# A projection's plain weight quarter in the tiles of the second sum, and a new order of the final norm's factors and the accumulators' additions

## The chip, the cores and the metric

One core of one Trainium2 chip runs the program alone. The metric is the device time in microseconds (us). Engines are named as in the profile: PE is TensorE, PEld its weight loads, DVE VectorE, ACT ScalarE, POOL GpSimd, SP SyncE, which only issues DMAs.

## What is computed

Two decoder layers on 512 tokens of width 1024, in float32: a pooling mixer and a latent attention of 16 heads, each with a SiLU gate and an output projection, plain residual additions, and one last RMSNorm. The change lies in the last projection and that norm:

```python
y = o.reshape(B, S, MLA_WIDTH) * jax.nn.silu(z)   # 512 x 2048
x = x + y @ w_out                                 # w_out: 2048 x 1024
return rmsnorm(x, final_norm)
```

## The kernel before

Every product of float32 matrices is made of three products of halves (`hi` and `lo`, a rounded part and the rest): `mm3` at L183 to L185. The halves of a weight strip come from ACT (`hi`, a copy) and DVE (`lo`, a subtraction): L166 and L167 for plain strips, L559 and L560 for summed ones, L188 and L189 for the activations.

The last projection is done in seven products instead of eight. `y` is cut into a11, a12, a21, a22 (two halves of the 2048 inner rows by two halves of the tokens), `w_out` into four quarters (two halves of the inner rows by LEFT and RIGHT columns). Some products take a quarter of `w_out` as it is, others a sum of quarters. Two objects of the class `Summed` hold these sums: `x_sum` in eight tiles (256 KB each) and `y_sum` in four (512 KB each). Their `load` fetches a quarter on SP's queue, or adds one to what the tiles hold, by an accumulating DMA on POOL's queue (L546). Their `strip(i)` makes the `hi` and `lo` of half a quarter. All strips, plain or summed, are cut from one ring of four buffers, two for a strip (`hi` and `lo`), so two strips live at a time. A plain strip (`columns_of`) goes through a ring of five `raw` buffers of 256 KB.

`products()` and `finish()`, under a hand-written order (`tc.manual_schedule()`), hold the work after the attention's last head, and the lines of each engine run in the order in which they stand. Ahead of them the heads' loop is put in order by the compiler's scheduler. One product (a11 with the plain upper LEFT quarter, into `acc`) is made in the heads' loop. Then six sets of products follow each other on PE; the first five are calls `multiply(banks, strips, slot, start)` of 48 matmuls, the last one is written out in `finish()` as calls of `part`:

1. both, with t1 (x_sum) and s1
2. last, with p2 (the plain quarter: lower half of the inner rows, LEFT) and a12
3. acc, with t2 (x_sum) and s2
4. both again, with y1 (y_sum) and s2 + a12
5. acc again, with y2 (y_sum) and s3
6. acc again, with t4 (x_sum) and a22

`acc`, `both` and `last` are pairs of PSUM banks, one bank for each of two token tiles. A later set adds to what a bank holds, so `gather` (L610, DVE), which adds a bank to the residual `xs`, must have read the bank between two sets. `split_rows` makes the halves of a part of y in `slots[0]` or `slots[1]`; `combine_rows` (L1055) forms s1, s2, s3.

y_sum's four tiles take the place of attention tiles: two `pm` buffers (the softmax's rows, last read by the transposes, L1022), `pt_hi` and `pt_lo` (last read by the values product, L183 to L185 and L1044). The output rows `o` later take the same four places.

The last norm: `square(t, c)` (ACT, L1210) sums the squares of half a token tile, `total` and `power` (POOL, L1218, L1226, L1227) make the factor `rs`, `normed` (DVE, L1233) multiplies and `send` stores on SP.

Of the kernel before, what the change touches and what calls it, by code (L numbers as in the profile page):

```python
# [11 lines left out]
F32 = mybir.dt.float32  # L12
# [3 lines left out]
ALU = mybir.AluOpType  # L16
# [34 lines left out]
def trunk_kernel(  # L51
# [514 lines left out]
    def columns_of(w, half, c, i):  # L566

        return strip([(w_rows(w, half * 8 + 4 * i, 4)[:, :, c], 4, 512)])[0]
# [32 lines left out]
    def multiply(banks, strips, slot, start, then=None):  # L601
        for q in range(2):
            for t in range(2):
                part(banks[t], strips[q], slot, q, t, start and q == 0, q == 1, not start)
                if then and q == 1:
                    then(t)

    def gather(t, c, b, op=ALU.add):

        dve.tensor_tensor(xs[:, t, c], xs[:, t, c], b, op)  # L610
# [420 lines left out]
    def values(h):  # L1031
        st, i2 = pairs[h // 2], h % 2
        c = slice(i2 * DN, (i2 + 1) * DN)
        b = bank()
        for j in range(NT - 1):
            n = S - j * P
            mm3(
                b[:, j * P :],
                tuple(v[:, j, c] for v in st["v"]),
                tuple(t[:, PT_BASE[j] : PT_BASE[j] + n] for t in (pt_hi, pt_lo)),  # L1040
                j == 0,
                False,
            )
        pe.matmul(b[:, S - P :], st["v3"][:, c], pt_3, start=False, stop=True)  # L1044
        dve.tensor_tensor(y[:, h, :], b, y[:, h, :], ALU.mult)
# [7 lines left out]
    def combine_rows(out, a, b, op, k0, k1):  # L1053
        for k in range(k0, k1, 2):
            dve.tensor_tensor(*(v[:, k : k + 2, :] for v in (out, a, b)), op)  # L1055

    def split_rows(src, slot, k0, k1):
        halves(*(v[:, k0:k1, :] for v in (src, *slot)))
# [14 lines left out]
    def first_sum(k0, k1):  # L1073
# [2 lines left out]
        x_sum.load(0, LEFT, pieces=range(k0, k1))  # L1076
        x_sum.load(0, RIGHT, add=True, pieces=range(k0, k1))

    (k0, q0), (k1, q1), vs = projections(0)
    qr = {1: QRope(1)}  # L1080
    k0()
# [10 lines left out]
    for h in range(H):  # L1092
        p, odd = divmod(h, 2)
        g, t = divmod(h + 5, 4)
        if h == 12:
            slots[1] = slot_of((lp, "t2"), (lp, "q_r"))
            first_half[0] = columns_of(w_out2, 0, LEFT, 0)
            split_rows(a11, slots[1], 0, 4)
            acc = [bank() for _ in range(2)]
        if h == 13:  # L1100
            split_rows(a11, slots[1], 4, 8)
        nxt = scores(h + 1) if h + 1 < H else None
        if h == 13:
            first_sum(0, 7)
        if h == 14:
            first_sum(7, 8)
        if odd:
            ahead = projections(p + 2) if p + 2 < H // 2 else [[], [], []]
        transposes(sc[0])
        if nxt:  # L1110
            softmax(*nxt)
        if units[odd]:
            units[odd][0]()
        if units[odd]:
            units[odd][1]()
        if h >= 12:
            q, t_ = divmod(h - 12, 2)
            part(acc[t_], first_half[q], slots[1], q, t_, q == 0, q == 1, False)
        if h == 14:
            slots[0] = slot_of((lp, "latT_hi"), (wk, "q_r"))  # L1120
            s1 = lp.tile([P, 8, 256], F32, name="s1", tag="latT_lo", bufs=1)
            combine_rows(s1, a21, a22, ALU.subtract, 0, 6)
            split_rows(s1, slots[0], 0, 4)
        if h == 15:
            t1 = [x_sum.strip(0)]
            split_rows(s1, slots[0], 4, 6)
        values(h)
        if g < 4 and t < 2:
            if t == 0:
                qr[g] = QRope(g)  # L1130
            qr[g].half(t)
            if t == 1:
                qr[g].turn()
        if odd:
            for u in units[2]:
                u()
            units = ahead
        if h == 13:
            first_half[1] = columns_of(w_out2, 0, LEFT, 1)
        sc = nxt  # L1140
# [3 lines left out]
    combine_rows(a21, a11, a21, ALU.subtract, 0, 6)  # L1144
    combine_rows(a11, s1, a11, ALU.subtract, 0, 6)
    s3, s2 = a21, a11
    y_sum.tiles = [
        ap.tile([P, 2, S], F32, name="b_y", tag=tag, bufs=n)
        for tag, n in (("pm", 2), ("pm", 2), ("pt_hi", 1), ("pt_lo", 1))
    ]  # L1150
    both = [bank() for _ in range(2)]
    last = [bank() for _ in range(2)]
    g_fin = row(final_norm, D, "g_fin", tag="gain")
# [1 line left out]
    def products():  # L1155

        combine_rows(s1, a21, a22, ALU.subtract, 6, 8)
        split_rows(s1, slots[0], 6, 8)
        x_sum.load(1, RIGHT, add=True, pieces=range(4))
        t1.append(x_sum.strip(1))  # L1160
        x_sum.load(1, RIGHT, add=True, pieces=range(4, 8))
        multiply(both, t1, slots[0], True)
        split_rows(a12, slots[1], 0, 4)
        p2 = [columns_of(w_out2, 1, LEFT, 0)]
        split_rows(a12, slots[1], 4, 8)
        p2.append(columns_of(w_out2, 1, LEFT, 1))
        y_sum.load(1, RIGHT)
        multiply(last, p2, slots[1], True)
        for t in range(2):
            gather(t, LEFT, acc[t])  # L1170
            gather(2 + t, RIGHT, both[t])
        combine_rows(s3, a11, a21, ALU.subtract, 6, 8)
        combine_rows(s2, s1, a11, ALU.subtract, 6, 8)
        split_rows(s2, slots[0], 0, 4)
        split_rows(s2, slots[0], 4, 8)
        t2 = x_sum.strips()
        x_sum.load(1, LEFT, add=True)
        multiply(acc, t2, slots[0], False)
        for i in (0, 4):
            combine_rows(s2, s2, a12, ALU.add, i, i + 4)  # L1180
            split_rows(s2, slots[1], i, i + 4)
        y1 = [y_sum.strip(0)]
        for t in range(2):
            gather(t, LEFT, last[t])
        y1.append(y_sum.strip(1))
        y_sum.load(0, RIGHT, add=True)
        multiply(both, y1, slots[1], False)
        for t in range(2):
            gather(t, RIGHT, acc[t], ALU.subtract)
        split_rows(s3, slots[0], 0, 4)  # L1190
        split_rows(s3, slots[0], 4, 8)
        y2 = [y_sum.strip(0)]
        for t in range(2):
            gather(t, RIGHT, both[t])
        y2.append(y_sum.strip(1))
        multiply(acc, y2, slots[0], False)
        split_rows(a22, slots[1], 0, 4)
        split_rows(a22, slots[1], 4, 8)

    o = [  # L1200
        ap.tile([P, D], F32, name="o", tag=tag, bufs=n)
        for tag, n in (("pm", 2), ("pm", 2), ("pt_hi", 1), ("pt_lo", 1))
    ]
    junk = lp.tile([P, 512], F32, name="junk", tag="k_a", bufs=1)
    ssq = {t: [] for t in range(NT)}
    rs = {}
# [1 line left out]
    def square(t, c):  # L1208
        r = sm.tile([P, 1], F32, name="ssq", tag="ssq8", bufs=12)
        act.activation(  # L1210
            junk[:, : c.stop - c.start], xs[:, t, c], AF.Square, scale=D**-0.5, accum_out=r
        )
        ssq[t].append(r)

    def total(t):

        r = sm.tile([P, 1], F32, name="total")
        pool.tensor_scalar(r, ssq[t][0], EPS, None, ALU.add)  # L1218
        for q in ssq[t][1:]:
            pool.tensor_tensor(r, r, q, ALU.add)  # L1220
        ssq[t] = [r]

    def power(t):

        rs[t] = sm.tile([P, 1], F32, name="rs")
        pool.tensor_tensor(rs[t], ssq[t][1], ssq[t][0], ALU.add)  # L1226
        pool.tensor_tensor(rs[t], rs[t], mhalf, ALU.pow)  # L1227
# [16 lines left out]

    def finish():

        t4 = [x_sum.strip(0)]
        for t in range(2):
            square(t, LEFT)
            total(t)  # L1250
            square(t, RIGHT)
            power(t)
            for c in (LEFT, RIGHT):
                normed(t, c)
        for t in range(2):
            gather(2 + t, RIGHT, acc[t], ALU.subtract)
            square(2 + t, RIGHT)
            part(acc[t], t4[0], slots[1], 0, t, False, False, True)
        t4.append(x_sum.strip(1))
        part(acc[0], t4[1], slots[1], 1, 0, False, True, True)  # L1260
        gather(2, LEFT, acc[0])
        total(2)
        square(2, LEFT)
        gained(3, RIGHT)
        c0, c1 = slice(0, 256), slice(256, 512)
        part(acc[1][:, c0], t4[1], slots[1], 1, 1, False, True, True, c0)
        power(2)
        rest = bank()[:, c0]
        part(rest, t4[1], slots[1], 1, 1, True, True, False, c1)
        gather(3, LEFT, acc[1])  # L1270
        square(3, c0)
        total(3)
        normed(2, LEFT)
        gather(3, c1, rest)
        square(3, c1)
        power(3)
        normed(2, RIGHT)
        scaled(3, RIGHT, act)
        normed(3, LEFT)
# [42 lines left out]
```

## Time and profile before

| | us |
|---|---|
| median of 3 runs | 725.84 |
| lowest and highest of the runs | 725.80, 726.76 |
| profiled execution, its own time | 725.06 |
| span of the profiled execution | 723.3 |
| PE busy | 704.1 (97% of the span) |
| DVE busy | 444.9 (62%) |
| ACT busy | 348.0 (48%) |
| POOL busy | 138.4 (19%) |

Times in the views count from the start of the span. A busy time of PE counts a matmul from its start to its modelled end, and neighbours overlap; so the distance from start to start tells the rate, and the brackets of the timeline the waits. In a bracket stands how long the engine was idle and what released it.

### The profile page before, as it was taken

Reading aid. Unit: us, or ns where it says so; the run is one execution under the profiler, and the core shown is the slowest. Engines: PE = TensorE matmul, PEld = TensorE weight load, DVE = VectorE, ACT = ScalarE, POOL = GpSimd, SP = SyncE. Lnnn points to the kernel's source line nnn. Section 1 sums busy time; section 2 is a strip of 40 time slices with the busy share of each in tenths; the row PEclk is TensorE's granted clock in tenths of the full one; section 3 lists DMA queues with packets and bytes.
Section 4 is the critical chain, followed back from the end, with each engine's and each line's share of the span. In section 5 each row is a group of like instructions: output and inputs, shape, how many; then the busy total and the mean of one; then the engine's idle time right before and its main releaser. Section 6 shows DMA issues by size and latency. Waiting matters only on the chain.

```text
span 723.3 us, 10067 instructions
## 1 busy us (share of the span) xinstructions
PE 704.1 (97%) x3529; PEld 601.6 (83%) x3529; DVE 444.9 (62%) x870; ACT 348.0 (48%) x752; POOL 138.4 (19%) x182
## 2 busy tenths in 40 slices
PE   7999999999999999999999999999999999998976
PEld 7888888888888888799888888989888988986855
DVE  5964453463577897642724212776876876897873
ACT  6452242242244566545733234574575565644561
POOL 5000000000001450145500023222032211132321
PEclk9999999999999999999999999999999999999988
DMA  7342341331355996135333523132141447367921
GB/s 258 121 135 62 114 117 60 116 112 63 117 180 115 245 184 138 48 110 152 104 102 80 145 66 102 52 78 67 45 128 52 96 124 175 89 107 203 173 84 59
DMA packets 69539, 82.79 MB, mean 114 GB/s; under 512 B 12144, under 2 KB 45936, under 8 KB 69488
## 3 DMA queue, kind: packets, MB, share of 16 engines
q1 hardware_dynamic: 60448, 65.10, 30.0%
q0 software_dynamic: 8896, 16.78, 13.5%
q8 instruction: 28, 0.46, 0.3%
q10 hardware_dynamic: 144, 0.26, 0.1%
q14 instruction: 23, 0.19, 0.1%
HBM read 75.83 MB, written 2.10 MB: 108 GB/s over the span
## 4 chain that ended last, share of the span: by engine, by line
PE 88%; issue 4%; POOL 3%; DMA 2%; DVE 1%; ACT 1%; POOLq 0%; SPq 0%; ACTq 0%; DVEq 0%
PE bank L183 26%; PE bank L184 26%; PE bank L185 26%; PE bank L1022 2%; PE bank L301 2%; POOL b_x L546 1%; PE bank L986 1%; PE bank L985 1%; DMA b_y<-in_mla_w_out 1%; PE bank L226 1%; PE bank L1044 0%; PE bank L988 0%; DMA xs<-in_x 0%; PE bank L271 0%; POOL b_y L546 0%
## 5 line engine op out<-in xcount | busy, mean ns | idle before, releaser
L166 ACT ACTIVATE w_hi<-raw 128x512 fp32r<-128x512 f32 (+2 forms) x200 | 105.0, 578 | 140.3 <-PE bank L184 121.5
L167 DVE TENSOR_TENSOR w_lo<-raw,w_hi 128x512 fp32r<-128x512 f32 x132 | 86.8, 690 | 118.4 <-ACT w_hi L166 117.6
L183 PE MATMUL bank<-h_hi,w_hi 128*128 128x512 f32 x368 | 143.4, 390 | 0.0
L185 PE MATMUL bank<-h_lo,w_hi 128*128 128x512 f32 x368 | 143.2, 389 | 0.0
L184 PE MATMUL bank<-h_hi,w_lo 128*128 128x512 f32 x368 | 143.2, 389 | 0.0
L167 POOL TENSOR_TENSOR w_lo<-raw,w_hi 128x256 fp32r<-128x256 f32 (+2 forms) x68 | 61.4, 928 | 174.5 <-ACT w_hi L166 171.4
L185 PEld LDWEIGHTS bank<-h_lo,w_hi 128*128 128x128 f32 x368 | 69.1, 188 | 14.4
L183 PEld LDWEIGHTS bank<-h_hi,w_hi 128*128 128x128 f32 x368 | 69.1, 188 | 14.3
L184 PEld LDWEIGHTS bank<-h_hi,w_lo 128*128 128x128 f32 x368 | 69.1, 188 | 14.3
L183 PE MATMUL bank<-w_hi,h_hi 128*128 128x512 f32 (+1 forms) x176 | 64.6, 367 | 0.0
L184 PE MATMUL bank<-w_hi,h_lo 128*128 128x512 f32 (+1 forms) x176 | 64.1, 364 | 0.0
L185 PE MATMUL bank<-w_lo,h_hi 128*128 128x512 f32 (+1 forms) x176 | 64.1, 364 | 0.0
L183 PE MATMUL bank<-w_hi,a_hi 128*128 128x512 f32 (+1 forms) x116 | 46.3, 399 | 7.1 <-DVE xs L610 5.1
L185 PE MATMUL bank<-w_lo,a_hi 128*128 128x512 f32 (+1 forms) x116 | 46.1, 397 | 0.6 <-DVE w_lo L560 0.6
L184 PE MATMUL bank<-w_hi,a_lo 128*128 128x512 f32 (+1 forms) x116 | 45.7, 394 | 0.0
L183 PE MATMUL bank<-latT_hi,w_hi 128*128 128x512 f32 x104 | 42.4, 408 | 0.0
L184 PE MATMUL bank<-latT_hi,w_lo 128*128 128x512 f32 x104 | 40.6, 391 | 0.0
L185 PE MATMUL bank<-latT_lo,w_hi 128*128 128x512 f32 x104 | 40.6, 390 | 0.0
L546 POOL DMA_DIRECT2D b_x<-in_mla_w_out x24 | 21.5, 1416 | 86.3 <-DVE w_lo L560 26.2
L560 DVE TENSOR_TENSOR w_lo<-b_x,w_hi 128x512 fp32r<-128x512 f32 (+1 forms) x40 | 33.9, 898 | 6.7 <-ACT w_hi L559 6.5
L185 PEld LDWEIGHTS bank<-w_lo,h_hi 128*128 128x128 f32 x176 | 33.0, 188 | 4.4
L183 PEld LDWEIGHTS bank<-w_hi,h_hi 128*128 128x128 f32 x176 | 33.0, 188 | 4.4
(204 smaller groups left out, 1405.5 us busy)
## 6 DMA issues: line engine op xcount, KB each, us to landing
raw<-in_pool_w_in SPq DMA_DIRECT2D x64, 256.0 KB, 3.1
raw<-in_mla_w_in SPq DMA_DIRECT2D x32, 256.0 KB, 3.2
b_x<-in_pool_w_out POOLq DMA_DIRECT2D x12, 512.0 KB, 8.2
b_x<-in_mla_w_out POOLq DMA_DIRECT2D x24, 256.0 KB, 6.0
raw<-in_mla_w_q_b SPq DMA_DIRECT2D x36, 128.0 KB, 2.3
raw<-in_pool_w_group SPq DMA_DIRECT2D x16, 256.0 KB, 2.6
q_r<-stack SPq DMA_DIRECT2D x64, 64.0 KB, 2.0
raw<-in_mla_w_kv_b SPq DMA_DIRECT2D x16, 256.0 KB, 3.0
```

The costliest lines, as they stand in the source:

```text
L166: act.activation(hi, raw, AF.Copy)
L167: ins = eng.tensor_tensor(lo, raw, f32(hi), ALU.subtract)
L183: pe.matmul(o, a[0], b[0], start=start, stop=False, skip_group_check=more)
L184: pe.matmul(o, a[1], b[0], start=False, stop=False, skip_group_check=more)
L185: pe.matmul(o, a[0], b[1], start=False, stop=stop, skip_group_check=more)
L226: pe.transpose(pt[:, i * P : (i + 1) * P], xn[:, k * P : (k + 1) * P], ident)
L301: pe.matmul(first[i][:, c], w0.views[0][a][:, k, i * P : (i + 1) * P], (h_hi, h_lo)[b][:, k, c], start=k == 0 and n == 0, stop=k == KD - 1 ...
L546: pool.dma_start(self.tiles[i], src, accum_op=ALU.add)
L560: eng.tensor_tensor(lv[:, k, :], raw, f32(hv[:, k, :]), ALU.subtract)
L985: pe.matmul(o, q_r[h // 4][:, h % 4, c], k_a[:, :n], start=True, stop=False)
L986: pe.matmul(o, q_r[h // 4][:, h % 4, c], k_b[:, :n], start=False, stop=False)
L1022: pe.transpose(b[:, n : n + P], pm[:, OFF[i] + j * P : OFF[i] + (j + 1) * P], ident)
```

## The change

`second_sum` is new. It makes y_sum's tiles in two steps, the two `pm` ones in the loop's last head and the two `pt` ones after the loop, and loads the plain quarter into them on SP. The second set's strips p2 come from `y_sum.strip` and no longer from `columns_of`; `y_sum.load(1, RIGHT)` stands behind them as before, and now overwrites the tiles that they were made from. In `products()` the combinations of rows 6 to 8 and the additions of `acc` move ahead of p2's second strip, and the additions of `both` move behind the split of s2. The squares, totals and powers of token tiles 0 and 1 move from `finish()` to two places in `products()`, one ahead of y2's first strip, one behind its second. In `finish()` the additions of `acc` to tokens 2 and 3 (RIGHT) and the first half of set 6 come first, then t4's second strip, then the normed rows of tokens 0 and 1. The tiles `o` are made at the start of `finish()`.

```diff
--- before.py
+++ after.py
@@ -1075,6 +1075,13 @@
             x_sum.tiles.append(home.tile([P, 1, S], F32, name="b_x", tag=tag, bufs=n))
         x_sum.load(0, LEFT, pieces=range(k0, k1))
         x_sum.load(0, RIGHT, add=True, pieces=range(k0, k1))
+
+    def second_sum(tags):
+
+        n = len(y_sum.tiles)
+        for tag, bufs in tags:
+            y_sum.tiles.append(ap.tile([P, 2, S], F32, name="b_y", tag=tag, bufs=bufs))
+        y_sum.load(1, LEFT, pieces=range(n, n + 2))
 
     (k0, q0), (k1, q1), vs = projections(0)
     qr = {1: QRope(1)}
@@ -1124,6 +1131,7 @@
         if h == 15:
             t1 = [x_sum.strip(0)]
             split_rows(s1, slots[0], 4, 6)
+            second_sum((("pm", 2), ("pm", 2)))
         values(h)
         if g < 4 and t < 2:
             if t == 0:
@@ -1144,10 +1152,7 @@
     combine_rows(a21, a11, a21, ALU.subtract, 0, 6)
     combine_rows(a11, s1, a11, ALU.subtract, 0, 6)
     s3, s2 = a21, a11
-    y_sum.tiles = [
-        ap.tile([P, 2, S], F32, name="b_y", tag=tag, bufs=n)
-        for tag, n in (("pm", 2), ("pm", 2), ("pt_hi", 1), ("pt_lo", 1))
-    ]
+    second_sum((("pt_hi", 1), ("pt_lo", 1)))
     both = [bank() for _ in range(2)]
     last = [bank() for _ in range(2)]
     g_fin = row(final_norm, D, "g_fin", tag="gain")
@@ -1161,18 +1166,19 @@
         x_sum.load(1, RIGHT, add=True, pieces=range(4, 8))
         multiply(both, t1, slots[0], True)
         split_rows(a12, slots[1], 0, 4)
-        p2 = [columns_of(w_out2, 1, LEFT, 0)]
+        p2 = [y_sum.strip(0)]
         split_rows(a12, slots[1], 4, 8)
-        p2.append(columns_of(w_out2, 1, LEFT, 1))
+        combine_rows(s3, a11, a21, ALU.subtract, 6, 8)
+        combine_rows(s2, s1, a11, ALU.subtract, 6, 8)
+        for t in range(2):
+            gather(t, LEFT, acc[t])
+        p2.append(y_sum.strip(1))
         y_sum.load(1, RIGHT)
         multiply(last, p2, slots[1], True)
-        for t in range(2):
-            gather(t, LEFT, acc[t])
-            gather(2 + t, RIGHT, both[t])
-        combine_rows(s3, a11, a21, ALU.subtract, 6, 8)
-        combine_rows(s2, s1, a11, ALU.subtract, 6, 8)
         split_rows(s2, slots[0], 0, 4)
         split_rows(s2, slots[0], 4, 8)
+        for t in range(2):
+            gather(2 + t, RIGHT, both[t])
         t2 = x_sum.strips()
         x_sum.load(1, LEFT, add=True)
         multiply(acc, t2, slots[0], False)
@@ -1189,18 +1195,21 @@
             gather(t, RIGHT, acc[t], ALU.subtract)
         split_rows(s3, slots[0], 0, 4)
         split_rows(s3, slots[0], 4, 8)
+        for t in range(2):
+            square(t, LEFT)
+            total(t)
         y2 = [y_sum.strip(0)]
         for t in range(2):
             gather(t, RIGHT, both[t])
         y2.append(y_sum.strip(1))
+        for t in range(2):
+            square(t, RIGHT)
+            power(t)
         multiply(acc, y2, slots[0], False)
         split_rows(a22, slots[1], 0, 4)
         split_rows(a22, slots[1], 4, 8)
 
-    o = [
-        ap.tile([P, D], F32, name="o", tag=tag, bufs=n)
-        for tag, n in (("pm", 2), ("pm", 2), ("pt_hi", 1), ("pt_lo", 1))
-    ]
+    o = []
     junk = lp.tile([P, 512], F32, name="junk", tag="k_a", bufs=1)
     ssq = {t: [] for t in range(NT)}
     rs = {}
@@ -1244,19 +1253,17 @@
 
     def finish():
 
+        for tag, n in (("pm", 2), ("pm", 2), ("pt_hi", 1), ("pt_lo", 1)):
+            o.append(ap.tile([P, D], F32, name="o", tag=tag, bufs=n))
         t4 = [x_sum.strip(0)]
         for t in range(2):
-            square(t, LEFT)
-            total(t)
-            square(t, RIGHT)
-            power(t)
+            gather(2 + t, RIGHT, acc[t], ALU.subtract)
+            part(acc[t], t4[0], slots[1], 0, t, False, False, True)
+        t4.append(x_sum.strip(1))
+        for t in range(2):
             for c in (LEFT, RIGHT):
                 normed(t, c)
-        for t in range(2):
-            gather(2 + t, RIGHT, acc[t], ALU.subtract)
             square(2 + t, RIGHT)
-            part(acc[t], t4[0], slots[1], 0, t, False, False, True)
-        t4.append(x_sum.strip(1))
         part(acc[0], t4[1], slots[1], 1, 0, False, True, True)
         gather(2, LEFT, acc[0])
         total(2)
```

## Rows read from the trace of the kernel before

**Rows 1.** Timeline, PE: start us, us, engine line op tiles, count, [idle before, releaser].

```profile
662.05 0.50 PE L183 MATMUL bank<-w_hi,a_hi 128*128 128x512 f32 x1 [2.00 <-ACT w_hi L559]
...
663.39 0.80 PE L185 MATMUL bank<-w_lo,a_hi 128*128 128x512 f32 x1 [0.61 <-DVE w_lo L560]
...
666.42 0.40 PE L183 MATMUL bank<-w_hi,a_hi 128*128 128x512 f32 x1
...
669.87 0.39 PE L183 MATMUL bank<-w_hi,a_hi 128*128 128x512 f32 x1
...
702.69 0.77 PE L183 MATMUL bank<-w_hi,a_hi 128*128 128x512 f32 x1 [5.14 <-DVE xs L610]
...
707.40 0.40 PE L185 MATMUL bank<-w_lo,a_hi 128*128 128x512 f32 x1
```

**Rows 2.** Busy time by stretch: stretch, its us, each engine, granted clock, DMA share, GB/s.

```profile
663.00:664.00 1.00, 0.61 (x2) 0.51 (x3) 1.00 (x3) 1.00 (x4) 0.36 (x1) 0.50 0.00 0
...
706.00:707.00 1.00, 1.00 (x4) 0.81 (x3) 1.00 (x2) 0.19 (x1) 0.00 (x0) 0.50 0.00 0
```

**Rows 3.** Timeline, ACT (ScalarE), 640 to 665.

```profile
648.94 0.63 ACT L166 ACTIVATE w_hi<-raw 128x512 fp32r<-128x512 f32 x1 [0.79 <-PE bank L184]
654.04 1.84 ACT L166 ACTIVATE w_hi<-raw 128x512 fp32r<-128x512 f32 x3 [4.47 <-DMA raw<-in_mla_w_out]
...
660.42 1.06 ACT L188 ACTIVATE a_hi<-y 128x1024 fp32r<-128x1024 f32 x1 [3.59 <-DVE y L1055]
661.38 3.73 ACT L559 ACTIVATE w_hi<-b_x 128x512 fp32r<-128x512 f32 x7
```

**Rows 4.** Timeline, DVE (VectorE), 640 to 676.

```profile
645.14 1.23 DVE L189 TENSOR_TENSOR a_lo<-y,a_hi 128x1024 fp32r<-128x1024 f32 x1
...
656.53 2.47 DVE L610 TENSOR_TENSOR xs<-xs,bank 128x512 f32<-128x512 f32 x4
...
660.25 2.49 DVE L189 TENSOR_TENSOR a_lo<-y,a_hi 128x1024 fp32r<-128x1024 f32 x2
662.65 4.89 DVE L560 TENSOR_TENSOR w_lo<-b_x,w_hi 128x512 fp32r<-128x512 f32 x8
667.47 1.28 DVE L1055 TENSOR_TENSOR y<-y 128x512 f32<-128x512 f32 x2
...
674.64 2.35 DVE L560 TENSOR_TENSOR w_lo<-b_y,w_hi 128x1024 fp32r<-128x1024 f32 x2
```

**Rows 5.** Timeline, PE, the last uses of the attention tiles.

```profile
634.87 0.93 PE L1022 MATMUL bank<-ident,pm 128*128 128x128 f32 x7
...
638.49 0.38 PE L1044 MATMUL bank<-pt,v 128*128 128x128 f32 x2
```

**Rows 6.** DMA issues in 648 to 662: form, count, KB each, median us to landing.

```profile
b_y<-in_mla_w_out SPq DMA_DIRECT2D x4, 512.0 KB, 8.7
raw<-in_mla_w_out SPq DMA_DIRECT2D x2, 256.0 KB, 6.9
```

**Rows 7.** Timeline, ACT (ScalarE), from 688.

```profile
690.67 1.06 ACT L559 ACTIVATE w_hi<-b_y 128x1024 fp32r<-128x1024 f32 x1 [1.40 <-DMA b_y<-in_mla_w_out]
691.63 1.99 ACT L188 ACTIVATE a_hi<-y 128x1024 fp32r<-128x1024 f32 x2
...
695.61 0.62 ACT L1210 ACTIVATE junk<-xs 128x512 f32<-128x512 f32 x1
696.13 0.19 ACT L1210 ACTIVATION_READ_ACCUMULATOR junk<-xs 128x1 f32 x1
```

**Rows 8.** Timeline, DVE (VectorE), from 690.

```profile
695.17 2.49 DVE L560 TENSOR_TENSOR w_lo<-b_x,w_hi 128x512 fp32r<-128x512 f32 x4
...
700.54 1.41 DVE L1233 SCALAR_TENSOR_TENSOR o<-xs,rs,g_fin 128x512 f32<-128x512 f32 x2 [0.73 <-POOL rs L1227]
701.87 1.28 DVE L610 TENSOR_TENSOR xs<-xs,bank 128x512 f32<-128x512 f32 x2
```

**Rows 9.** Timeline, POOL (GpSimd), 670 to 690.

```profile
676.15 1.22 POOL L546 DMA_DIRECT2D b_y<-in_mla_w_out  x1 [5.41 <-DVE w_lo L560]
```

## The prediction, made before the changed kernel was run

> **What bounds the kernel now.** I read the page first, then the timeline of each engine over the last projection, then the clock by stretch. TensorE is busy 97% of the span (the table above), so time can only come from the few places where it waits. The PE timeline of the last projection has two that matter [rows 1]. The reader is to see the brackets: 2.00 us idle before the product at 662.05 (ended by ScalarE's w_hi), with 0.61 us more before 663.39, and 5.14 us idle before 702.69 (ended by an xs addition on VectorE). Each also drags the clock down: the granted clock is 0.50 (1.2 GHz) at 663 to 664 and at 706 to 707 [rows 2].
>
> Price of the first wait: from 666.42 to 669.87 fifteen products start 0.23 apart, at full clock; from 662.05 to 666.42 nine took 4.37 instead of 2.07. With the 2.00 that is 4.3 us; with the overlap of one product's tail, 4.5 [rows 1]. Price of the second: 5.14 idle, and eleven products from 702.69 to 707.40 at 0.43 instead of 0.23, 2.2 us [rows 1].
>
> What causes the first: the third product set (`multiply(acc, t2)`) waits for t2's w_hi at 661.38, which on ScalarE stands behind the split at 660.42, which waited 3.59 us for a VectorE combination [rows 3]. That combination stands behind four additions of accumulators at 656.53, and these behind the plain quarter's second strip, whose `raw` buffers landed only for 654.04, after a 4.47 us wait [rows 3, 4]. TensorE needed none of those additions then. So the root is a late plain load, and an order on VectorE that puts other work ahead of the split.
>
> What causes the second: product set five ends at 697.55, and the sixth goes on into the same banks, so it first needs `gather(2, RIGHT, acc[0])`. In VectorE's order that stands behind the normed rows of tokens 0 and 1, and these behind four squares on ScalarE and two powers on GpSimd, so it runs at 701.87 [rows 7, 8].
>
> **The change part by part.** *Plain quarter to y_sum's tiles.* Gone are eight 256 KB `raw` loads; four of 512 KB come instead, the same bytes. Tile 0 waits for the pm buffer of head 14, tile 1 for the last transposes (635.80), tiles 2 and 3 for the last values product (638.87) [rows 5]. On SP nothing is queued behind them but the later `y_sum.load(1, RIGHT)` and the output's stores. They are first read by ScalarE at about 645 (tile 0), 646 (tile 1) and 649 (tiles 2, 3). Time to land is bounded from rows by 8.7 us, the median of the same 512 KB form under full DMA load, above [rows 6], and nothing below: tile 1 by 644.5, the others by 647.6. So the load is hidden at either end, and I cost it at nothing; if it lands later than that, ScalarE waits, and all that follows on it.
>
> Here a rule of the Trainium skill speaks ("DMA: Bandwidth & Descriptors", section "Queues, rings and completion order"): each DMA engine takes turns between the queues that have work, so a load on SP's queue would get its share at once beside GpSimd's accumulating loads. The trace shows more than a small delay: 256 KB raw loads took 6.9 us beside them [rows 6]. By the page the late-tile rival below would have almost no chance; I keep it.
>
> The price of this part is that `y_sum.load(1, RIGHT)`, before free to go at once, now waits for the p2 strips to be read (VectorE, some 648 to 654). With 8.7 us it lands by 663 [rows 6]; y1's first strip reads it near 669. Hidden.
>
> *Strips 1024 wide.* Splitting a b_y tile costs VectorE 2.35 for two, ScalarE 1.06 each, against 0.61 for each 512-wide piece [rows 4, 7]: the same work.
>
> *VectorE's new order.* Up to the split at 645.14 nothing is changed [rows 4]. From there, by the widths of [rows 4]: split 1.23, p2's first strip 2.35, split 1.23, two combinations 1.28, two additions 1.24, second strip 2.35, the two halves of s2 2.46, two additions 1.24, t2's eight pieces 4.89; sum 18.3, ending at 663.4. Before they ended at 667.54. That is 4.1; since neighbours overlap by up to 0.08 there, some 0.3 more: 4.4 us. A strip's buffers come free only when TensorE has read the strip two before it (the 0.79 wait at 648.94 shows that) [rows 3], so t2's second strip cannot start on ScalarE before 660; its four pieces still fit. t2's first piece is ready near 659, before TensorE ends the second set at 660.05. So the first wait goes, TensorE gains its 4.4, and what is late next is y1's first w_lo, which moves with VectorE by the same 4.4 and so stays within 0.2 of TensorE.
>
> *Accumulating loads.* The b_y loads of the second sum are released by y1's w_lo (GpSimd waits 5.41 for it at 676.15) [rows 9]. They move by 4.4 too; the last one, which ScalarE waits for until 690.67 [rows 7], is then due at 686.3.
>
> *Squares and factors.* The LEFT squares go to ScalarE's wait for the first b_y tile, hidden there; totals and powers on GpSimd follow the last b_y issue there and hold up nothing. The two RIGHT squares stand between the last b_y copy and the split of a22: 2 x (0.62 + 0.19) = 1.6 us on the path [rows 7].
>
> *The end.* From the last landing: copy 1.06, squares 1.6, first half of a22 1.0 [rows 7], then on VectorE two halves 2.46 [rows 4], t4's first strip 2.49, one addition 0.64 [rows 8]; sum 9.25. Before, landing to resumption took 702.69 - 690.67 = 12.0. So 2.8 less, on top of the 4.4: TensorE resumes at 695.5, and its wait shrinks from 5.14 to some 2.5. The normed rows (1.41 for two [rows 8]) follow the additions and t4's second strip, while TensorE has 5.5 us of work; they cost nothing. From there to the end the order is as before.
>
> *The clock.* A wait of 2.5 us is not one the trace shows. Nearest is the first, 2.00 and 0.61, which dropped the clock and cost seven products 0.2 each, 1.4 us; bounds are 0 and the 2.2 of the 5.14 wait. I take 1.4, so 0.8 less than now.
>
> **Sum.** 4.4 + 2.8 + 0.8 = 8.0 us. The profiled execution took 725.06 (span 723.3 and 1.76 around it), 0.8 under the median of the three runs: 725.06 - 8.0 = 717.0 us.
>
> **Rivals.**
> - *The short wait leaves the clock at 2.4 GHz.* 1.4 more: 715.6. For it: the wait is half the old one and dense work follows. Against: 2.00 us was enough at 662.
> - *The accumulating loads do not move.* The later second-sum loads collide with x_sum's accumulations, and the last b_y tile lands as late as before. Then only the end's 2.8 and 0.8 remain: 721.4. For it: 512 KB takes 8.7 us under load [rows 6]. Against: the plain bytes before it now move in idle stretches.
> - *The second wait stays at its length* because the squares on ScalarE take back what the earlier addition gives, or another wait on VectorE does. Only the first gain is left: 725.06 - 4.4 = 720.7. Against: the sum of rows above leaves 2.8.
> - *Late plain tiles, slower.* Tile 1 or tiles 2 and 3 land behind the accumulating loads. Each us after 646 (tile 1) or 649 holds ScalarE, VectorE and then TensorE from its second set on, and pushes back `y_sum.load(1, RIGHT)` too. It takes all 8.0 back when tile 1 lands at 654, where the `raw` pieces landed before [rows 3]; at 657 it is 728. Against: tile 1 may be issued at 635.8, 18 us before that [rows 5].
> - *Nothing changes*, because the loads or the order do not come out as written: 725.
>
> **How the numbers follow.** Forecast 0.48 (717.0), clock stays up 0.25 (715.6), loads do not move 0.12 (721.4), second wait stays 0.06 (720.7), nothing 0.04, late tiles 0.05 (728). The range leaves out the last two and part of the rest: 714.6 (the second case with 1 us to spare) to 721.4; the likeliest two alone span 715 to 718.5. About 0.2%, 1.45 us, is what a measurement here can tell from no change. Faster by more than that 0.91, within it 0.04, slower 0.05.
>
> **What would show it.** In the profile after: no PE idle of over 0.5 us between 640 and 690; no `raw` on ScalarE after 640; t2's w_hi split in two groups, the second near 660; the last wait for a b_y landing ending near 686; one PE wait of 2 to 3 us, ended by an xs addition, near 693 to 696; and a clock of 0.50 for a few us after it, or not. Wrong would be a wait for b_y near 646 to 650, or a last b_y landing near 690.

## The result, and the profile after

| | before | after |
|---|---|---|
| median, us | 726.18 (4 runs, 725.80 to 726.76) | 716.82 (4 runs, 715.48 to 717.67) |
| profiled execution, us | 725.06 | 715.48 |
| its span, us | 723.3 | 713.6 |

The ratio is 0.9869, with a 95% interval of 0.985 to 0.9887: by the ratio some 9.5 us less, and the medians are 9.4 apart. 717.0 was forecast, 8.0 less than the profiled execution before.

The changed kernel's waits of PE from 600 us to the end, as a view (who waited for whom: total us, times, longest), are one line. Before there were three, [rows 1].

```profile
PE bank L183 <- DVE xs L610: 1.9, 1, 1.9
```

The PE timeline of the changed kernel around that wait, columns as in [rows 1]:

```profile
693.20 0.39 PE L185 MATMUL bank<-w_lo,a_hi 128*128 128x512 f32 x1
695.44 0.47 PE L183 MATMUL bank<-w_hi,a_hi 128*128 128x512 f32 x1 [1.85 <-DVE xs L610]
695.75 0.39 PE L184 MATMUL bank<-w_hi,a_lo 128*128 128x512 f32 x1
```

Set five's last matmul starts at 693.20, and set six at 695.44 after 1.85 us idle, where it had been 5.14. The matmul behind it starts 0.31 later, the next ones 0.23 apart. The clock after the wait, by stretch (columns as in [rows 2]), did not fall in this execution:

```profile
694.00:695.00 1.00, 0.00 (x0) 0.00 (x0) 1.00 (x3) 1.00 (x4) 0.00 (x0) 1.00 0.00 0
...
697.00:698.00 1.00, 1.00 (x6) 0.82 (x5) 1.00 (x3) 0.00 (x0) 0.00 (x0) 1.00 0.00 0
```

ACT in the changed kernel, columns as in [rows 3] and [rows 7]:

```profile
645.63 1.99 ACT L559 ACTIVATE w_hi<-b_y 128x1024 fp32r<-128x1024 f32 x2
...
649.55 2.01 ACT L559 ACTIVATE w_hi<-b_y 128x1024 fp32r<-128x1024 f32 x2 [0.98 <-PE bank L184]
...
655.04 2.19 ACT L559 ACTIVATE w_hi<-b_x 128x512 fp32r<-128x512 f32 x4 [1.58 <-issue]
660.43 2.20 ACT L559 ACTIVATE w_hi<-b_x 128x512 fp32r<-128x512 f32 x4 [3.20 <-PE bank L184]
...
686.52 1.06 ACT L559 ACTIVATE w_hi<-b_y 128x1024 fp32r<-128x1024 f32 x1 [1.40 <-DMA b_y<-in_mla_w_out]
687.48 0.61 ACT L1219 ACTIVATE junk<-xs 128x512 f32<-128x512 f32 x1
...
688.85 2.00 ACT L188 ACTIVATE a_hi<-y 128x1024 fp32r<-128x1024 f32 x2
```

No `raw` strip is left here. The second plain strip (649.55) waits for PE to give back its buffers, not for a DMA as at 654.04 in [rows 3]. t2 comes in two groups, 655.04 and 660.43, the second again held by PE's buffers. The last b_y tile is read at 686.52 (690.67 in [rows 7]), then come the squares, then a22.

DVE, columns as in [rows 4] and [rows 8]:

```profile
651.64 1.28 DVE L610 TENSOR_TENSOR xs<-xs,bank 128x512 f32<-128x512 f32 x2
652.83 2.35 DVE L560 TENSOR_TENSOR w_lo<-b_y,w_hi 128x1024 fp32r<-128x1024 f32 x2
655.10 2.35 DVE L189 TENSOR_TENSOR a_lo<-y,a_hi 128x1024 fp32r<-128x1024 f32 x2
657.38 1.28 DVE L610 TENSOR_TENSOR xs<-xs,bank 128x512 f32<-128x512 f32 x2
658.57 5.03 DVE L560 TENSOR_TENSOR w_lo<-b_x,w_hi 128x512 fp32r<-128x512 f32 x8
...
689.93 2.36 DVE L189 TENSOR_TENSOR a_lo<-y,a_hi 128x1024 fp32r<-128x1024 f32 x2 [1.09 <-ACT a_hi L188]
692.21 2.49 DVE L560 TENSOR_TENSOR w_lo<-b_x,w_hi 128x512 fp32r<-128x512 f32 x4
694.61 1.28 DVE L610 TENSOR_TENSOR xs<-xs,bank 128x512 f32<-128x512 f32 x2
...
703.88 0.69 DVE L610 TENSOR_TENSOR xs<-xs,bank 128x512 f32<-128x512 f32 x1 [2.94 <-PE bank L185]
```

t2's eight pieces start at 658.57 and end at 663.60, where they ended at 667.54 [rows 4]. The additions for set six run at 694.61, directly behind t4's first strip; before, 4.2 us lay between (697.66 to 701.87), 2.8 of them normed rows and the rest waits for their factors [rows 8].

Where the 9.7 us of span went, from marks that both traces have:

| mark | before | after | difference |
|---|---|---|---|
| last values product (L1044) starts | 638.49 | 639.11 | +0.62 |
| last matmul of set five starts | 697.16 | 693.20 | -3.96 |
| set six starts | 702.69 | 695.44 | -7.25 |
| `gather(2, LEFT)` starts | 713.33 | 703.88 | -9.45 |
| end of the span | 723.3 | 713.6 | -9.7 |

Against the first mark, the front gave 4.6, the last wait 3.3, and the stretch after it, 8.44 us long instead of 10.64, another 2.2. The 0.62 is not the change's: a difference of this size is there right at the start, where the product behind the last of the first transposes (L271) starts at 18.80 us before and at 19.52 after.

### The profile page after: what moved, and what is told of

Read it like the earlier page. It is cut to its first block, busy times and chain, and to the rows that moved or that the text cites. A ratio compares the mean times of both kernels' runs of the same rounds, so it can differ in the third digit from the quotient of the medians.

```text
span 713.6 us, 10044 instructions
## 1 busy us (share of the span) xinstructions
PE 700.9 (98%) x3529; PEld 600.6 (84%) x3529; DVE 444.4 (62%) x866; ACT 347.5 (49%) x748; POOL 137.5 (19%) x182
## 4 chain that ended last, share of the span: by engine, by line
PE 94%; DMA 2%; DVE 1%; issue 1%; ACT 1%; POOL 0%; POOLq 0%; SPq 0%; ACTq 0%; DVEq 0%
PE bank L184 28%; PE bank L183 28%; PE bank L185 28%; PE bank L1022 2%; PE bank L301 2%; PE bank L986 1%; PE bank L985 1%; DMA b_y<-in_mla_w_out 1%; PE bank L226 1%; PE bank L271 1%; PE bank L988 0%; PE bank L1044 0%; DMA xs<-in_x 0%; ACT junk L1219 0%; DVE a_lo L189 0%
## 5 line engine op out<-in xcount | busy, mean ns | idle before, releaser
L166 ACT ACTIVATE w_hi<-raw 128x512 fp32r<-128x512 f32 (+2 forms) x192 | 100.4, 576 | 135.6 <-PE bank L184 121.2
L167 DVE TENSOR_TENSOR w_lo<-raw,w_hi 128x512 fp32r<-128x512 f32 x124 | 81.7, 691 | 114.6 <-ACT w_hi L166 113.9
L183 PE MATMUL bank<-w_hi,a_hi 128*128 128x512 f32 (+1 forms) x116 | 44.7, 385 | 1.9 <-DVE xs L610 1.9
L185 PE MATMUL bank<-w_lo,a_hi 128*128 128x512 f32 (+1 forms) x116 | 44.5, 384 | 0.0
L559 ACT ACTIVATE w_hi<-b_x 128x512 fp32r<-128x512 f32 (+1 forms) x40 | 29.7, 794 | 19.4 <-DMA b_x<-in_pool_w_out 7.5
```

Source lines behind the costliest of these rows:

```text
L166: act.activation(hi, raw, AF.Copy)
L167: ins = eng.tensor_tensor(lo, raw, f32(hi), ALU.subtract)
L183: pe.matmul(o, a[0], b[0], start=start, stop=False, skip_group_check=more)
L185: pe.matmul(o, a[0], b[1], start=False, stop=stop, skip_group_check=more)
L559: act.activation(hv[:, k, :], raw, AF.Copy)
```

## The experiments

Each experiment is a version of one of the two kernels. Medians stand with the count of runs. Ratios are to the kernel before, run beside the version on the same chip: its median was 726.27, and 725.92 beside the third square and the last two profiles of the changed kernel. A gain in us is worked out from the ratio.

### Each part alone

*The front alone.* The changed kernel with `finish()` as before and without the squares in `products()`:

```diff
-        for t in range(2):
-            square(t, LEFT)
-            total(t)
         y2 = [y_sum.strip(0)]
...
-        for t in range(2):
-            square(t, RIGHT)
-            power(t)
```

> The front alone: the plain quarter in y_sum's tiles and VectorE's new order in the second set, with the squares, powers and additions of the end as before the change. Theory (the two waits are priced apart): the first wait of 2.00 us goes, 4.4 us less, 721.8 beside a median of 726.2; the last wait stays near 5.1 us with the clock at 0.50 after it. Rival (one gain hangs on the other): under 2 us less, over 724.

Measured: 720.57 (4 runs), ratio 0.993 (0.9914 to 0.9947), or 5.1 us. PE, around the last wait:

```profile
699.10 0.77 PE L183 MATMUL bank<-w_hi,a_hi 128*128 128x512 f32 x1 [5.35 <-DVE xs L610]
```

The first wait is gone and the last one is as long as it was, 5.35. The theory holds; the gain is 0.7 over the 4.4 expected, within the interval (3.8 to 6.2 us). Some of it is the clock: the stretch from the start of set six to `gather(2, LEFT)`, which starts at 709.21 here, is 10.11 us long and was 10.64 before, though the wait ahead of it is no shorter.

*The end alone.* The kernel before, with the squares and `finish()` of the changed one. The same lines as above are added to the kernel before, and its `finish()` gets the order of the change.

> The end alone: squares, factors and additions in the new order, the plain quarter and VectorE's order in the second set as before the change. Theory: the first wait stays at 2.00 us; last landing to resumption shrinks from 12.0 to 9.3, the last wait to some 2.3 us; 2.8 less, and 0.8 to 2.2 more from the clock: 721.2 to 722.6 beside 726.2. Rival (without the front the end brings nothing, since the landing of the last b_y tile decides): 725 to 726.

Measured: 721.79 (4 runs), ratio 0.9939 (0.9915 to 0.9963), or 4.4 us. PE:

```profile
663.10 0.50 PE L183 MATMUL bank<-w_hi,a_hi 128*128 128x512 f32 x1 [1.98 <-ACT w_hi L559]
...
664.44 0.80 PE L185 MATMUL bank<-w_lo,a_hi 128*128 128x512 f32 x1 [0.61 <-DVE w_lo L560]
...
700.72 0.47 PE L183 MATMUL bank<-w_hi,a_hi 128*128 128x512 f32 x1 [2.15 <-DVE xs L610]
```

The first wait is where it was, 1.98 and 0.61, and the last one has shrunk to 2.15, with 2.3 expected. So the end does not need the front. 5.1 and 4.4 add up to 9.5, the whole gain, as two independent parts would, though with 1.2 and 1.7 us either way the times alone would not show it. The traces do: from the last values product (L1044) t2 ends on DVE after 24.49 us with the front alone and in the whole change, and from the last landing to set six it takes 8.92 us with the end alone and in the whole change.

### In the front: the load or the order

*The load alone.* The front, with VectorE's order as before:

```diff
-        combine_rows(s3, a11, a21, ALU.subtract, 6, 8)
-        combine_rows(s2, s1, a11, ALU.subtract, 6, 8)
-        for t in range(2):
-            gather(t, LEFT, acc[t])
         p2.append(y_sum.strip(1))
         y_sum.load(1, RIGHT)
         multiply(last, p2, slots[1], True)
+        for t in range(2):
+            gather(t, LEFT, acc[t])
+            gather(2 + t, RIGHT, both[t])
+        combine_rows(s3, a11, a21, ALU.subtract, 6, 8)
+        combine_rows(s2, s1, a11, ALU.subtract, 6, 8)
         split_rows(s2, slots[0], 0, 4)
         split_rows(s2, slots[0], 4, 8)
-        for t in range(2):
-            gather(2 + t, RIGHT, both[t])
```

> The load alone: the plain quarter in y_sum's tiles, VectorE's order as before the change (all four additions, then the combinations, behind p2's second strip). Theory (the late raw load is the cause, the order does no harm once it is gone): VectorE ends t2's pieces near 663, as in the front alone; time equal to the front alone within 0.5 us, near 721.8. Rival (the order is the cause): little gain, 724 to 726.

Measured: 721.26 (4 runs), ratio 0.9937 (0.992 to 0.9954), or 4.6 us. ACT and DVE:

```profile
649.42 2.01 ACT L559 ACTIVATE w_hi<-b_y 128x1024 fp32r<-128x1024 f32 x2 [0.99 <-PE bank L184]
```

```profile
652.80 2.47 DVE L610 TENSOR_TENSOR xs<-xs,bank 128x512 f32<-128x512 f32 x4
655.19 0.68 DVE L1055 TENSOR_TENSOR y<-y 128x512 f32<-128x512 f32 x1
655.90 0.69 DVE L1055 TENSOR_TENSOR y<-s,y 128x512 f32<-128x512 f32 x1
656.51 2.49 DVE L189 TENSOR_TENSOR a_lo<-y,a_hi 128x1024 fp32r<-128x1024 f32 x2
658.93 4.90 DVE L560 TENSOR_TENSOR w_lo<-b_x,w_hi 128x512 fp32r<-128x512 f32 x8
```

ACT takes the second plain strip at 649.42, held by PE's buffers and not by a DMA, DVE goes through the four additions, the combinations and the splits without a stop, and t2 ends at 663.83. The four additions ahead of the combinations, which stood on the path before, cost PE nothing here but a wait of 0.36 at y1.

*The order alone.* The kernel before, with the combinations and additions moved as in the change, and p2 still through `raw`.

> VectorE's new order alone, the plain quarter through raw as before the change. Theory (the late raw load is the cause): ScalarE still waits for raw until 654, VectorE ends t2's pieces near 665.1 instead of 667.5, TensorE then waits 0.4 us at the third set and 1.6 at the fourth; 2.4 us less, 723.8. Rival (the order is the cause): the full 4.4 less, 721.8.

Measured: 723.36 (6 runs), ratio 0.9961 (0.9945 to 0.9977), or 2.8 us. ACT, DVE and PE:

```profile
653.49 1.89 ACT L166 ACTIVATE w_hi<-raw 128x512 fp32r<-128x512 f32 x3 [4.17 <-DMA raw<-in_mla_w_out]
```

```profile
659.82 4.89 DVE L560 TENSOR_TENSOR w_lo<-b_x,w_hi 128x512 fp32r<-128x512 f32 x8
```

```profile
660.56 0.50 PE L185 MATMUL bank<-w_lo,a_hi 128*128 128x512 f32 x1 [0.35 <-DVE w_lo L560]
...
671.63 0.50 PE L183 MATMUL bank<-w_hi,a_hi 128*128 128x512 f32 x1 [0.37 <-ACT w_hi L559]
...
673.08 0.50 PE L185 MATMUL bank<-w_lo,a_hi 128*128 128x512 f32 x1 [0.72 <-DVE w_lo L560]
```

ACT still waits 4.17 us for `raw`. DVE ends t2 at 664.71, and PE waits 0.35 at the third set (660.56) and 0.37 and 0.72 at the fourth, where 1.6 had been expected. The times of the two runs have intervals that overlap (3.3 to 5.8 us for the load, 1.7 to 4.0 for the order); the traces tell them apart. From the last values product, t2 ends on DVE 4.2 us earlier than before with the load alone, 2.6 with the order alone, and 4.6 with both. As expected of the late load as the cause: the order buys a part of what the load buys, and little on top of it.

*The plain tiles later in the program.* The changed kernel with the lines that make all four tiles behind the heads' loop:

```diff
-            second_sum((("pm", 2), ("pm", 2)))
...
+    second_sum((("pm", 2), ("pm", 2)))
     second_sum((("pt_hi", 1), ("pt_lo", 1)))
```

> The changed kernel with all four plain tiles issued behind the heads' loop, tiles 0 and 1 included. Theory (the load is hidden): the DMA engines are idle from 639 on, 2 MB at the 0.34 MB per us of rows after take 6 us, tile 1 lands by 644 and tile 3 by 647, no time is lost. Rival (late plain tiles): ScalarE waits for b_y near 646, up to 3 us more.

Measured: 717.25 (4 runs), beside 717.99 (5 runs) of the changed kernel. ACT:

```profile
645.82 1.99 ACT L559 ACTIVATE w_hi<-b_y 128x1024 fp32r<-128x1024 f32 x2
...
649.75 2.01 ACT L559 ACTIVATE w_hi<-b_y 128x1024 fp32r<-128x1024 f32 x2 [0.98 <-PE bank L184]
```

No wait for a DMA at either strip. But the loads did not start later. SP's issue of the second tile, first in this run and then in the changed kernel:

```profile
636.64 0.38 SPq L548 DMA_DIRECT2D b_y<-in_mla_w_out  x1
```

```profile
636.44 0.38 SPq L548 DMA_DIRECT2D b_y<-in_mla_w_out  x1
```

The four issues stand at 628.44, 636.64, 639.38 and 639.84 here and at 628.25, 636.44, 639.18 and 639.64 there, 0.2 later each, and so is the last values product (639.31 against 639.11). The lines moved and the loads did not, so this run is no test of late plain tiles; what they would cost was not measured.

### The last wait and the clock

*The changed kernel again*, in three more profiles.

> The changed kernel again, for its spread. If the wait of 1.85 us drops the clock in some executions and not in others, the runs lie in two groups, near 715.5 with a mean granted clock of 0.998 and near 717 with less; if the spread has another cause, time and clock do not go together.

> The changed kernel once more, for the clock behind the last wait, of which two profiles so far say different things (1.85 us idle and no fall; 2.05 us and a fall that cost 1.6). If the length near 2 us decides, a profile with 1.9 us or less keeps 2.4 GHz and one with 2.0 or more falls; if not, the two do not go together.

> As the one before it: one more profile of the changed kernel for the same question.

Measured: 717.99 (5 runs), 716.36 (4 runs) and 718.29 (1 run). The first and the third of these profiles, PE and then one stretch behind the wait:

```profile
695.74 0.47 PE L183 MATMUL bank<-w_hi,a_hi 128*128 128x512 f32 x1 [2.05 <-ACT w_hi L559]
```

```profile
698.00:699.00 1.00, 1.00 (x4) 0.72 (x4) 1.00 (x2) 0.00 (x0) 0.68 (x1) 0.50 0.00 0
```

```profile
696.68 0.47 PE L183 MATMUL bank<-w_hi,a_hi 128*128 128x512 f32 x1 [2.24 <-DVE xs L610]
```

```profile
699.00:700.00 1.00, 1.00 (x4) 0.71 (x4) 1.00 (x2) 0.00 (x0) 0.62 (x1) 0.50 0.00 0
```

The waits were 2.05, 2.23 and 2.24 us, and in all three the clock went to 0.50 (1.2 GHz) 0.3 to 1.4 us after PE had gone on (in stretches of 0.1 us, at 697.1, 696.2 and 698.0). From the start of set six to `gather(2, LEFT)` it took 10.06, 10.09 and 10.10 us, against 8.44 in the profile where it did not fall. A fall costs 1.6 us. The length of the wait fits all four, of which the one of 1.85 us kept its clock, and the run above with the moved lines, which waited 2.03 us and fell; but a line between 1.85 and 2.03 rests on one profile below it.

What goes with a longer or shorter wait can be read from the same profiles. From ACT's read of the last b_y tile to set six it takes the same time in all of them; what differs is how long the first of the four accumulating loads takes, from its issue on POOL to its read on ACT:

| profile | first accumulating load, us | last read to set six, us | wait, us | clock behind it |
|---|---|---|---|---|
| changed kernel, as in the result | 6.75 | 8.92 | 1.85 | stays |
| moved lines (above) | 6.92 | 8.92 | 2.03 | falls |
| changed kernel again, first | 6.92 | 8.93 | 2.05 | falls |
| changed kernel again, second | 7.56 | 8.92 | 2.23 | falls |
| changed kernel again, third | 7.58 | 8.93 | 2.24 | falls |

Run by run the times do not split into two groups, and time and mean granted clock do not go together (717.67 had 0.996, 716.37 had 0.994). So the spread has other causes too. Part of it is there before the last projection, whose first mark, the last values product, lies at 638.81 to 639.55 us in the four profiles. The mean also holds the start: eight transposes there took 1.97 us in the changed kernel's profile and 1.09 in another kernel's (with the early split, below), nearly the ratio of the clock's two levels, while the clock column gives 1.00 for both and so cannot be trusted there:

```profile
6.58 1.97 PE L271 MATMUL bank<-ident,xn 128*128 128x128 f32 x8 [0.82 <-DVE xn L264]
```

```profile
7.06 1.09 PE L271 MATMUL bank<-ident,xn 128*128 128x128 f32 x8 [1.71 <-DVE xn L264]
```

*A third square.* The changed kernel with one more square ahead of the split of a22, its result unused:

```diff
         for t in range(2):
             square(t, RIGHT)
             power(t)
+        square(0, RIGHT)
         multiply(acc, y2, slots[0], False)
```

> The changed kernel with a third square (one of tokens 0, RIGHT, made again and not used) between the last b_y copy and the split of a22. Theory (ScalarE's squares lie one for one on the chain): the last wait grows by 0.75 us to 2.7, the clock falls in the profile, and the median is 0.8 us over the changed kernel's, more if that one keeps its clock in some executions. Rival (VectorE's work hides a square): no change.

Measured: 718.02 (4 runs), beside 716.36 of the changed kernel. ACT and PE:

```profile
687.12 1.06 ACT L559 ACTIVATE w_hi<-b_y 128x1024 fp32r<-128x1024 f32 x1 [1.40 <-DMA b_y<-in_mla_w_out]
...
690.21 1.99 ACT L188 ACTIVATE a_hi<-y 128x1024 fp32r<-128x1024 f32 x2
```

```profile
696.80 0.47 PE L183 MATMUL bank<-w_hi,a_hi 128*128 128x512 f32 x1 [3.03 <-DVE xs L610]
```

From the last b_y copy to set six it takes 9.68 us, against 8.92 after the change: 0.76 more, one square. The wait is 3.03, the clock falls, and from set six to `gather(2, LEFT)` it takes 10.09 as with the waits of 2.05 to 2.24. So ACT's squares lie one for one on the chain, and the fall costs the same for a wait of 2 or of 3 us. The medians are 1.7 apart; 0.8 of that is the square, and the rest may be runs of the changed kernel that kept their clock, which is not shown.

*The RIGHT squares behind t4's first strip*:

```diff
         y2.append(y_sum.strip(1))
-        for t in range(2):
-            square(t, RIGHT)
-            power(t)
         multiply(acc, y2, slots[0], False)
...
         t4 = [x_sum.strip(0)]
+        for t in range(2):
+            square(t, RIGHT)
+            power(t)
```

> The changed kernel with the two RIGHT squares and the powers moved behind t4's first strip. Theory (the squares cost 1.4 us on the chain from the last landing, and the last wait is what drops the clock): the wait shrinks from 1.85 to 0.4 us, 1.4 us less when the clock stays up in both, 714.1, and no run with a lower clock; median 2 us under the changed kernel's. Rival (VectorE's order alone sets the wait): no change.

Measured: 715.18 (4 runs), ratio 0.9845 (0.9825 to 0.9865), 2.8 us under the changed kernel run beside it. PE and DVE:

```profile
694.27 0.47 PE L183 MATMUL bank<-w_hi,a_hi 128*128 128x512 f32 x1 [1.05 <-ACT w_hi L559]
```

```profile
687.62 1.23 DVE L560 TENSOR_TENSOR w_lo<-b_y,w_hi 128x1024 fp32r<-128x1024 f32 x1 [1.23 <-ACT w_hi L559]
688.77 2.35 DVE L189 TENSOR_TENSOR a_lo<-y,a_hi 128x1024 fp32r<-128x1024 f32 x2
691.03 2.49 DVE L560 TENSOR_TENSOR w_lo<-b_x,w_hi 128x512 fp32r<-128x512 f32 x4
693.45 1.28 DVE L610 TENSOR_TENSOR xs<-xs,bank 128x512 f32<-128x512 f32 x2
```

The wait shrank to 1.05, not to 0.4: from the last landing to set six it takes 7.74 us, 1.2 less. DVE has no idle time left in it from 687.62 to the addition at 693.45, so it and no longer ACT sets the end of the wait. (The bracket names ACT, as that of 2.05 us above does. By the kernel's lines set six begins with t4's first strip, whose copies ACT had ended by 691.6, and needs the addition at 693.45; the copy named is one for t4's second strip that ended at about the same time.) The clock stays up, in the profile as in the mean of all four runs (0.997 and 0.998). The 1.2 and the fall of 1.6 that the changed kernel's profile beside it had make the 2.8.

*And half of a22 split early*:

```diff
+        split_rows(a22, slots[1], 0, 4)
         y2.append(y_sum.strip(1))
         multiply(acc, y2, slots[0], False)
-        split_rows(a22, slots[1], 0, 4)
         split_rows(a22, slots[1], 4, 8)
```

> The same, and the first half of a22 is split ahead of y2's second strip. Theory: from the last landing only one half stands ahead of t4's strip, 1.1 us less on VectorE; the last wait goes, and TensorE runs through: 0.4 us under the kernel with late squares, 713.7. Rival: the earlier split delays y2's third tile, and TensorE waits in set five instead: no gain or a loss of up to 1 us.

Measured: 713.92 (5 runs), ratio 0.9825 (0.9804 to 0.9846), or 12.7 us under the kernel before. PE's only wait in the last projection:

```profile
685.15 0.50 PE L185 MATMUL bank<-w_lo,a_hi 128*128 128x512 f32 x1 [0.23 <-DVE w_lo L560]
```

The last wait is gone. What the rival said is there too, but small: 0.23 us at the third piece of y2. The median lies 1.3 us under the kernel with late squares, more than the 0.4 expected and about the 1.05 of the wait that went; the two intervals overlap. This version beats both kernels.

## Why the prediction was right

*Size.* That 717.0 meets the median of 716.82 so closely is in part luck. The 8.0 us were taken off one execution of 725.06, which lay 1.1 under the median of its kernel, 726.18; the medians are 9.4 apart, 1.4 more than forecast. In the traces the sum fares better. From the last values product to `gather(2, LEFT)` it took 74.84 us before; in the three profiles of the changed kernel whose clock fell, the forecast case, it took 8.3, 7.7 and 7.6 less, and 10.1 less in the one whose clock stayed up. Why the median of the kernel before lies over its profile is not shown.

*The first wait.* Predicted 4.4 us, with t2 ending on VectorE at 663.1 to 663.4; measured 4.6 against the first mark, ending at 663.60 with everything 0.62 late. The prediction named two causes, a late load and an order, and did not weigh them. The runs do: of the 4.6 by which t2 ends earlier, the load alone gives 4.2 and the order alone 2.6, so the load is nearly enough by itself.

*The load at no cost.* The bound was 8.7 us to land. The DMA view of the changed kernel in 626 to 641 (columns as in [rows 6]) has the plain tiles:

```profile
b_y<-in_mla_w_out SPq DMA_DIRECT2D x4, 512.0 KB, 5.0
```

5.0 us in the median. Tile by tile, from the issues at 628.25, 636.44, 639.18 and 639.64, the loads took 3.9, 6.0, 4.6 and some 5.4 us; tile 1 landed at 642.4 and the last near 645.0, and ACT read them at 645.63 and 649.55, 3.2 and 4.5 us later. So it was right to cost the load at nothing. The 8.7 was a safe end and too long, and the chance of 0.05 for late tiles stood on it.

The prediction saw that `raw` loads took 6.9 us beside accumulating ones. The trace of the kernel before shows more of it. SP issued the three of the second strip from 647.00 on, while accumulating loads that POOL had issued from 643.70 on were still moving. The issues, and then both queues in 647.0 to 650.5 (packets, MB, share of 16 engines), q0 POOL's and q1 SP's:

```profile
647.00 2.18 SPq L160 DMA_DIRECT2D raw<-in_mla_w_out  x3
```

```profile
q0 software_dynamic: 319, 0.58, 101.9%
q1 hardware_dynamic: 1, 0.00, 0.2%
```

SP's loads moved next to nothing until the accumulating ones had run down. In the changed kernel all four plain tiles have landed before most of that backlog is issued (644.31 on). The Trainium skill ("DMA: Bandwidth & Descriptors", section "Queues, rings and completion order") has the DMA engines take turns between the queues that have work. This trace does not agree: 319 packets against 1 in 3.5 us is no taking of turns, and the measurement decides. It bears out the doubt of the prediction, which kept its rival of late tiles against the Trainium skill's rule.

*The accumulating loads.* The last one was due at 686.3 and was read at 686.52. So they moved with VectorE, and the rival in which they stay is out.

*The end.* The sum gave 9.25 us from the last landing to set six; it took 8.92. The two squares were put at 1.6 and took 1.37 (687.48 to 688.85), 0.76 for one more in the run with a third. The wait was put at some 2.5, though 5.14 less the sum's own 2.8 is 2.3, and came out at 1.85 to 2.24: widths of rows added up overstate a chain by some hundredths for each neighbour.

*The clock.* This was the one step with a wide bound, 0 to 2.2, taken at 1.4. Of four profiles of the changed kernel three fell, at 1.6 each, and one did not. So the forecast case is the common one, and the rival of 715.6 is what the profiled execution (715.48) shows. The 0.8 to be won had set the 1.4 against the 2.2 of one profile. Where the clock fell it was some 0.55 (10.64 less 10.06 to 10.10), and the 2.2 is itself no fixed price of a long wait: with the front, the load and the order alone, PE was idle for 5.34 to 5.35 us and the stretch behind it took 10.11, 10.20 and 10.15 us, some 1.7 over the 8.44. Which of the two cases an execution takes hangs on some tenths of a microsecond of waiting, and these go with the time that the first accumulating load takes (6.75 to 7.58 us); what moves that time was not tried.

## What to carry to other kernels

Price each wait with the stretch at the lower clock behind it, and look for what makes a wait short enough to keep the clock: here 1.2 us off the chain behind the last landing, which took a wait of 2.05 to 1.05, were worth 2.8. When a late DMA and an order both stand ahead of a wait, run each alone; here the order's gain was nearly gone once the load was early. Before reading a run as a test of a later load, look up when the load was issued: moving its line moved nothing here. Where a chain starts at a landing, take everything off it that can go before the landing or behind the chain: two squares moved and one half split early gave some 4 us more than the change (713.92 beside 717.99).

## What the runs showed of the hardware

An idle time of TensorE of 2.0 to 3.0 us between dense stretches was followed by the clock of 1.2 GHz in every profile that had one (2.03, 2.05, 2.15, 2.23, 2.24 and 3.03 us; also 2.00 and 1.98 at the first wait, with 0.61 more behind it), and so was one of 5.1 to 5.4 us. 1.85 and 1.05 were not. The length of one wait is not the whole condition: at the start of the program, where the work comes in short groups, waits of 1.71 and 1.43 us in the kernel with the early split were followed by a clock of 0.50 from 11.6 to 15.0 us.

The price did not grow with the wait: 10.06 us to the next mark after 2.05 idle, 10.09 after 3.03 and 10.11 after 5.35, against 8.44 without a fall. Only the kernel before paid more after its 5.14, 10.64 us. There the clock fell at 700.4, 2.3 us before PE went on, and was up again at 707.3, 4.6 us behind; with the front alone it fell at 695.8, 3.3 us before PE went on, and was up again at 702.6, 3.5 us behind.

Plain loads on SP's queue stood still beside a backlog of accumulating loads on POOL's: 1 packet against 319 in 3.5 us before the change, where 256 KB took 6.9 us to land [rows 6], and 1 against 208 in the 2.1 us after the issue of the second plain tile in the changed kernel.
